# A hybrid attention and mLSTM encoder layer: background stores, weight sums and loads queued behind each projection's last evacuation and its store

## The chip, the cores and the metric

The kernel runs on one core of a Trainium2 chip. Five engines matter: TensorE (PE) multiplies matrices out of SBUF into PSUM, VectorE (DVE) and ScalarE (ACT) do elementwise work and empty PSUM, GpSimd (POOL) does a little, and SyncE (SP) issues nearly all DMAs between the device's memory (HBM) and SBUF. Each engine works through its own queue in order. The metric is the device time of one execution in microseconds (us).

## The reference

One encoder layer is applied to two sequences, a prompt of 1024 tokens and a sample of 2048, with 16 learned meta tokens in front, model width 1024. Cut to what matters here:

```python
xn = _rmsnorm(h, g_pre)
proj = xn @ w_in + b_in                       # 1024 x 6672, all float32
na_q, na_k, na_v, na_z, ml_qk, ml_v, ml_z, ml_o, ml_g, mg = split(proj)
ya = (neighbourhood_attention(na_q, na_k, na_v, na_rpb) * silu(na_z)) @ w_a
yb = (mlstm_branch(ml_qk, ml_v, ml_g, ml_o, ml_conv_w, ml_head_g) * silu(ml_z)) @ w_b
ga, gb = split(sigmoid(mg))
out = h + _rmsnorm((ga * ya + gb * yb) @ w_out, g_post)
```

## The kernel before, in words

**Numbers.** Float32 products are made of three passes: each operand is split into a high part (rounded by a copy on ScalarE) and a low part (the rest, by a subtraction on VectorE), and `mm3` (lines 182 to 187) issues high x high, low x high and high x low. For weights the parts are `whi` and `wlo`, for the normalised tokens `xh` and `xl`.

**Dense and sparse work.** The projections, the output stage and the gates are the dense stream (`dense`, line 1922); the mLSTM (`ml`) and the neighbourhood attention (`na`) are the sparse stream (`sparse`, line 1969). `run` interleaves the two, so that TensorE has projection matmuls to do while the other stream's chain of small steps goes on. The order of TensorE's instructions is that in which they are written. On all other engines the framework's scheduler chooses the order of each queue from a simulated timeline: an instruction that is written late but depends on nothing can stand early in its queue. `tc.issue_after(x)` limits that: what is written in its block on the engine of x is queued behind x. It adds an order of issue and no wait for a result.

**PLAN** (line 41) lists the groups of the dense stream: (sequence, first token, columns), columns m for the mLSTM's, n for the attention's, g for the gates'; the entries with f are the final stages. A group covers 1024 tokens in two halves of 512. `group` (line 936) works in jobs: four blocks of 128 columns, each by `fm_half` for the first half and then the second. `fm_half` (line 647) makes 24 matmuls into one PSUM bank (two banks with meta tokens) and yields four times; then `fm_evac` (line 600) empties the bank on VectorE and ScalarE into a tile `st` (4 buffers) and stores that to HBM from SP (lines 631 to 639). PSUM has three banks `pj` for this. `tm_unit` (line 676) does the same for columns whose tokens lie on partitions, two yields to a block.

**Turns.** After each yield of `group` and `sgates`, `beside` (line 523) counts a turn and does a piece of background work. A turn has 6 matmuls of 512 columns or 12 of 256. The first group takes 166 turns, the first two 298, the first three 458. The first job of the first group is the four columns of the mLSTM's q (tensors `mq`), turns 1 to 32; the second its gate z. Columns of z are evacuated by two ACT steps and one VectorE step (lines 620 to 622).

**Background work.**
- *Stores of x.* The sparse order of PLAN comes back to a half later, so `xkeep` (line 514) queues 16 stores of 256 KB for each half of 512 tokens, the eight slices of `xh` and of `xl`, in `xput`. `beside` issues one at every fourth turn (line 528). `xparts` (line 354) hands out new buffers for x; before that it issues all that is still in `xput` (line 356), since the buffers of the half before last are reused.
- *wprep* (line 537), the block sums of the gate weights. The gates of two groups are computed by a seven-product block scheme (`sgates`, line 859), which needs sums of blocks of the weights. For each of 8 pairs of column blocks wprep loads 2 x 512 KB of raw weights (`pr`, line 549), yields three times, and then four times makes a tile `po`: a copy on ACT (line 562), a subtraction on VectorE (line 563), two stores of 512 KB (tensors q, line 566), two yields; two of the four have VectorE sums before them and one more yield. `pr` and `po` have one buffer each. This is 13 steps to a pair, 104 in all. One step is taken at every second turn from turn 28, and at every eighth from the sixth pair on.
- *tprep* (line 570), block sums of x for the same scheme, in groups (1, 1024, n) and (1, 0, n): at every third turn a step of VectorE and ACT work on tiles `xr`, with stores to the tensors T.
- *tload* (line 837): six loads of 1 MB of T. In the gate group (1, 1024, g), `sgates` takes one at a time between its first projections.
- *build_half* (line 442) prepares the next half of x: loads of tokens (`xr`), sums of squares (line 331), loads of the transposed tokens (`xt`), the split. It isn't under `beside`.

`held` (line 167) looks up the last instruction written on VectorE and on ScalarE, of whatever kind, and queues its block behind these two. It surrounds the store of x in `beside`, and the loads of T in `sgates`; both are SP instructions. wprep and tprep run outside of it.

The weights themselves (`wload`, `wpump`, `wflush`, lines 249 to 307) come from `wu` at the first use, are split, and their two parts are stored (`wh`, `wl`); later groups load these.

Of the kernel before, what the change touches and what calls it, by code (L numbers as in the profile page):

```python
# [20 lines left out]
KT = D // P  # L21
# [114 lines left out]
class K:  # L136
# [3 lines left out]
    def __init__(self, tc, ins, outs):  # L140
        self.tc, self.nc = tc, tc.nc
        self.xs = []
        self.i, self.o = ins, outs
        self.wreq, self.wraw, self.wrdy, self.wout = deque(), deque(), deque(), 0
        self.wseen, self.wkept, self.xkept = set(), {}, {}
        self.rwait = {}
        self.xput, self.turn, self.last, self.turns = deque(), 0, None, False
        self.need = False
        self.hold, self.early = deque(), True
        self.side, self.qd, self.TD = None, {}, {}  # L150
# [15 lines left out]
    @contextmanager  # L166
    def held(self):

        with ExitStack() as st:
            left = {mybir.EngineType.DVE, mybir.EngineType.Activation}  # L170
            for x in reversed(self.nc.cur_bb.bb.instructions):
                if x.engine in left:
                    left.remove(x.engine)
                    st.enter_context(self.tc.issue_after(x))
                    if not left:
                        break
            yield

    def psum(self, tag, shape):
# [172 lines left out]
        self.nc.scalar.activation(out, p, AF.Copy)  # L352

    def xparts(self):
        while self.xput:
            self.nc.sync.dma_start(*self.xput.popleft())
        return [self.wp.tile([P, KT, HALF], F32R, name=n, bufs=2) for n in ("xh", "xl")]

# [83 lines left out]
    def build_half(self, s, t0, res):  # L442

        nc, wp = self.nc, self.wp
        if (s, t0) in self.xkept:
            yield
            yield "scaled"
            x = []
            for name, part in zip(("xh", "xl"), self.xkept[s, t0]):
                x.append(wp.tile([P, KT, HALF], F32R, name=name, bufs=2))  # L450
                for k in range(0, KT, 4):
                    nc.sync.dma_start(x[-1][:, k:k + 4, :512].bitcast(F32), part[:, k:k + 4, :])
                yield
            res.append(tuple(x))
            return
        if s == 0:
            xts = self.xnext
            self.xnext = None
            while self.rwait:
                yield "wait"  # L460
            self.early = False
            yield "scaled"
            g = self.gpre
            p = self.psum("sm", [P, 512])
            nc.tensor.matmul(p[:, :KT], self.ident, g, start=True, stop=True)
            g = self.cp.tile([P, KT], F32, name="gx")
            nc.vector.tensor_copy(g, p[:, :KT])
            x, r = self.xparts(), []
            for e in range(4):
                self.xsplit(x, xts[e], e, 0, g)  # L470
                self.wflush(2)
                yield
            res.append(tuple(x))
            self.xkeep(s, 0, self.xs[0], NM)
            self.xkeep(s, t0, x)
            yield from self.rsum(self.toks, r)
            nc.vector.tensor_copy(self.rc[:, 4:8], r[0])
            dg = self.rdiag(r[0], self.toks[0][0])

            def rows():  # L480
                self.rrows(dg, self.rr[:, 1], "sm")
                self.RD = self.dp.tile([P, D], F32, name="rrd")
                nc.sync.dma_start(self.RD[:, :], self.rr.rearrange("p a t -> p (a t)"))
                self.xp.close()
                self.side, self.pace = self.wprep(), 2
            self.rwait[s, t0] = rows
        else:
            bp = self.bp
            toks, r = self.tokens(s, t0, range(4), bp, 4), []
            yield  # L490
            yield from self.rsum(toks, r)
            dg = self.rdiag(r[0], toks[3][0])
            xts = [self.xtload(s, t0, e, bp, 4) for e in range(3)]
            yield
            rr = bp.tile([P, 512], F32, name="rx", tag="thT", bufs=1)
            self.rrows(dg, rr, "pj")
            xts.append(self.xtload(s, t0, 3, bp, 4))
            yield
            for k in range(KT):
                v = xts[k // 2][:, k % 2]  # L500
                nc.vector.scalar_tensor_tensor(v, v, self.gpre[:, k:k + 1], rr, op0=ALU.mult, op1=ALU.mult)
                if k % 2:
                    yield
            yield "scaled"
            x = self.xparts()
            for e in range(4):
                h = x[0][:, 2 * e:2 * e + 2, :512]
                nc.scalar.activation(h, xts[e], AF.Copy)
                nc.vector.tensor_tensor(x[1][:, 2 * e:2 * e + 2, :512], xts[e], h.bitcast(F32), op=ALU.subtract)
                yield  # L510
            res.append(tuple(x))
            self.xkeep(s, t0, x)
# [10 lines left out]
    def beside(self):  # L523

        self.turn += 1
        if self.xput and self.turn % 4 == 1:
            with self.held():
                self.nc.sync.dma_start(*self.xput.popleft())
        if self.side and self.turn % self.pace == 0 and next(self.side, "end") == "end":
            self.side = None  # L530

    def drain(self):
        while self.side:
# [3 lines left out]
    def wprep(self):  # L537

        nc = self.nc
# [2 lines left out]
        self.pq = ExitStack()  # L542
        pool = self.pq.enter_context(self.tc.tile_pool(name="pq", bufs=1, side="right", reuse_waits="tile"))
        for p in range(8):
            if p == 5:
                self.pace = 8
            raw = pool.tile([P, 2, 2, 512], F32, name="pr", bufs=1)
            for f in range(2):
                nc.sync.dma_start(raw[:, f].rearrange("p a c -> p (a c)"), self.i["wu"][unit["i", C_GA + (2 * p + f) * P, P], :, :D])
            for _ in range(3):  # L550
                yield
            for f, ops in ((0, ("11", "12")), (1, ("21", "22")), (1, ("s3", "s1")), (0, ("s2", "s4"))):
                if ops[0] == "s3":
                    nc.vector.tensor_tensor(raw[:, 1, 1], raw[:, 1, 0], raw[:, 1, 1], op=ALU.add)
                    sub(raw[:, 1, 0], raw[:, 0, 0], raw[:, 1, 0])
                    yield
                if ops[0] == "s2":
                    sub(raw[:, 0, 0], raw[:, 1, 1], raw[:, 0, 0])
                    sub(raw[:, 0, 1], raw[:, 0, 1], raw[:, 0, 0])
                    yield  # L560
                o = pool.tile([P, 2, 2, 512], F32R, name="po", bufs=1)
                nc.scalar.activation(o[:, :, 0], raw[:, f], AF.Copy)
                sub(o[:, :, 1], raw[:, f], o[:, :, 0].bitcast(F32))
                for q, op in enumerate(ops):
                    d = self.qd[p, op] = self.dp.tile([P, D], F32, name=f"q{p}{op}")
                    nc.sync.dma_start(d[:, :], o[:, q].rearrange("p a c -> p (a c)").bitcast(F32))
                yield
                yield
# [31 lines left out]
    def fm_evac(self, col, s, t0, meta, chunks, ps):  # L600

        nc, wp = self.nc, self.wp
        bi = (col // P) if col < 4608 else 36 + (col - 4624) // P
        bias = self.bfm[:, bi:bi + 1]
        st = wp.tile([P, HALF], F32, name="st", bufs=4)
        m = NM if meta else 0
        n = 512 + m
# [19 lines left out]
        if C_MQ <= col < C_MV:  # L627
            dst = (self.MQ if col < C_MK else self.MK)
            h = (col % 512) // P
            lo = 0 if meta else NM + t0  # L630
            nc.sync.dma_start(dst[s][h][:, lo:lo + n], st[:, :n])
            if meta:
                nc.sync.dma_start(dst[1 - s][h][:, :NM], st[:, :NM])
            return
        if col >= C_GA:
            dst = self.GT[s][(col - C_GA) // P]
        else:
            dst = (self.NQ, self.NK, None, self.NZ, None, None, None, self.SZ)[col // 512][s][(col % 512) // P]
        nc.sync.dma_start(dst[:, t0:t0 + 512], st[:, m:n])
        if meta and C_NK <= col < C_NV:  # L640
            km = wp.tile([P, 64], F32, name="km", bufs=1)
            nc.gpsimd.memset(km, 0.0)
# [33 lines left out]
    def tm_unit(self, col, halves, wd):  # L676
# [10 lines left out]
        for j, (x, s, c, n, cnt, tok) in enumerate(todo):  # L687
            st = self.bp.tile([P, 2, WU], F32, name="stT", bufs=4)
            for a in range(cnt):
# [17 lines left out]
                        yield (8 if tok is None else 12) * C256  # L707
                if j == len(todo) - 1 and a == cnt - 1:
                    self.wdone()
                if tok is None:  # L710
                    nc.scalar.activation(st[:n, 1, :wd], p[2 * NM:2 * NM + n, :wd], AF.Copy)
                    nc.vector.tensor_tensor(st[:n, 1, :wd], p[:n, :wd], st[:n, 1, :wd], op=ALU.add)
# [5 lines left out]
                    nc.vector.tensor_tensor(st[:n, a, :wd], p[:n, :wd], bb[:n, :wd], op=ALU.add)  # L718
                if a == cnt - 1:
                    self.tm_store(col, wd, s, n, cnt, tok, st)  # L720
                yield (8 if tok is None else 12) * C256

    def tm_store(self, col, wd, s, n, cnt, tok, st):
# [135 lines left out]
    def sgates(self, s, t0, lead, nxt):  # L859
# [3 lines left out]
        for hf in range(2):  # L863
            if hf == 0:
                ws = [self.wtake(1)[0] for _ in range(2 * len(lead))]
            for u, w in enumerate(ws):
                if hf or u > 1:
                    with self.held():
                        next(more, None)
                p, f = lead[u // 2], u % 2  # L870
                yield from self.fm_half(C_GA + (2 * p + f) * P, w, self.xs[hf], s, t0 + 512 * hf, False, done=self.wdone if hf else None)
# [1194 lines left out]
```

## Time and profile before

| | us |
|---|---|
| median of 3 runs | 2782.44 (2778.36 to 2783.21) |
| the profiled execution's own time | 2780.05 |
| its span (first to last instruction) | 2778.2 |
| TensorE busy in it | 2704.1 |
| VectorE busy | 1877.6 |
| ScalarE busy | 1388.7 |

The profile shows one execution. A row of instructions names the line, the engine, what is written and read (out<-in), how many (x), and how long the engine stood idle before it and what ended that idle time ([us <-releaser]). PEld is TensorE's loading of weights, which overlaps the matmuls. SPq, ACTq and DVEq are the engines' sequencers; SPq with DMA_DIRECT2D is the issue of a DMA, not its transfer. The DMA share is the mean busy share of the core's 16 DMA engines, and PEclk the clock that TensorE was granted, 1.00 being full speed. All places are in us from the start of the span.

### The profile page before, as it was taken

The page shows a single profiled execution, that of the slowest core. Times are in us where ns is not written, and L with a number is a line of the kernel's source. Part 1 is how long each engine was busy: PE and PEld are TensorE (multiplying, and loading weights), DVE is VectorE, ACT ScalarE, POOL GpSimd, SP SyncE. Part 2 cuts the span into 40 slices and gives each one's busy share as a digit, 9 for nine tenths or more (in the row PEclk, how much of TensorE's full clock was granted, in tenths as well). Part 3 has the DMA queues.
Part 4 walks back from the last instruction along what each step waited for, and adds up shares of the span by engine and source line. Part 5 has one row for each costly group of instructions (what it writes and reads, how often), then busy time and mean ns, then how long its engine had stood idle before and what let it go on. Part 6 is the DMA issues. An engine that isn't in the chain of part 4 may idle for free.

```text
span 2778.2 us, 47366 instructions
## 1 busy us (share of the span) xinstructions
PE 2704.1 (97%) x16144; PEld 2380.2 (86%) x16144; DVE 1877.6 (68%) x5174; ACT 1388.7 (50%) x3302; POOL 17.9 (1%) x100
## 2 busy tenths in 40 slices
PE   9699899999999999999999999999999999999998
PEld 7599798889878998898798887887888989899898
DVE  5343588866768666368867665674668798887844
ACT  5332464653446555346546564562455556555421
POOL 0000000000000000000000000000000000000000
PEclk9899999999999999999999999999999999999999
DMA  9978887965599655679969889989549898989975
GB/s 367 365 291 306 301 309 263 368 222 174 199 363 319 207 188 181 206 227 340 319 227 314 278 260 362 320 256 330 166 152 313 255 316 251 344 261 299 304 254 208
DMA packets 397539, 762.76 MB, mean 275 GB/s; under 512 B 50192, under 2 KB 179168, under 8 KB 395760
## 3 DMA queue, kind: packets, MB, share of 16 engines
q1 hardware_dynamic: 396176, 757.04, 80.1%
q0 software_dynamic: 1120, 2.69, 0.4%
q8 instruction: 128, 2.10, 0.3%
q14 instruction: 115, 0.94, 0.1%
HBM read 514.89 MB, written 244.69 MB: 273 GB/s over the span
## 4 chain that ended last, share of the span: by engine, by line
PE 50%; DMA 3%; DVE 2%; ACT 0%; issue 0%; SPq 0%; DVEq 0%; ACTq 0%
PE pj L185 7%; PE pj L187 7%; PE pj L186 7%; PE pj L1827 3%; PE pj L1829 3%; PE pj L1828 3%; PE pj L891 3%; PE pj L893 3%; PE pj L892 3%; PE sm L1176 2%; PE tr L1161 2%; DMA whi<-q 1%; PE pj L701 1%; PE pj L702 1%; PE pj L703 1%; DMA t2h<-t2h 0%
## 5 line engine op out<-in xcount | busy, mean ns | idle before, releaser
L185 PE MATMUL pj<-xh,whi 128*128 128x512 f32 (+1 forms) x1376 | 543.5, 395 | 29.4 <-ACT st L621 21.1
L186 PE MATMUL pj<-xl,whi 128*128 128x512 f32 (+1 forms) x1376 | 529.2, 385 | 0.4 <-DVE xl L366 0.4
L187 PE MATMUL pj<-xh,wlo 128*128 128x512 f32 (+1 forms) x1376 | 528.5, 384 | 0.8 <-DMA wlo<-wl 0.5
L701 PE MATMUL pj<-whi,xh 128*128 128x256 f32 (+1 forms) x1152 | 329.2, 286 | 0.0
L185 PEld LDWEIGHTS pj<-xh,whi 128*128 128x128 f32 x1376 | 263.0, 191 | 74.7 <-ACT st L621 21.6
L702 PE MATMUL pj<-wlo,xh 128*128 128x256 f32 (+1 forms) x1152 | 324.8, 282 | 0.0
L703 PE MATMUL pj<-whi,xl 128*128 128x256 f32 (+1 forms) x1152 | 324.7, 282 | 0.0
L187 PEld LDWEIGHTS pj<-xh,wlo 128*128 128x128 f32 x1376 | 261.9, 190 | 55.9 <-DMA wlo<-wl 1.6
L186 PEld LDWEIGHTS pj<-xl,whi 128*128 128x128 f32 x1376 | 262.9, 191 | 41.8 <-issue 1.0
L1827 PE MATMUL pj<-whi,mh 128*128 128x256 f32 x768 | 217.2, 283 | 0.4 <-DMA whi<-wh 0.4
L701 PEld LDWEIGHTS pj<-whi,xh 128*128 128x128 f32 x1152 | 217.0, 188 | 0.4
L702 PEld LDWEIGHTS pj<-wlo,xh 128*128 128x128 f32 x1152 | 217.0, 188 | 0.1
L703 PEld LDWEIGHTS pj<-whi,xl 128*128 128x128 f32 x1152 | 217.0, 188 | 0.0
L1829 PE MATMUL pj<-whi,mlo 128*128 128x256 f32 x768 | 216.8, 282 | 0.0
L1828 PE MATMUL pj<-wlo,mh 128*128 128x256 f32 x768 | 216.7, 282 | 0.0
L1168 DVE TENSOR_TENSOR pts<-tr,pts 96x384 fp32r<-96x384 f32 (+2 forms) x192 | 118.8, 619 | 70.5 <-ACT pts L1163 68.9
L1163 ACT ACTIVATE pts<-tr 96x384 fp32r<-96x384 f32 (+2 forms) x192 | 103.4, 539 | 106.9 <-PE tr L1161 106.0
L185 PE MATMUL pj<-yh,whi 128*128 128x512 f32 x384 | 154.9, 403 | 0.0
L187 PE MATMUL pj<-yh,wlo 128*128 128x512 f32 x384 | 151.3, 394 | 0.0
L186 PE MATMUL pj<-yl,whi 128*128 128x512 f32 x384 | 150.8, 393 | 0.0
L1827 PEld LDWEIGHTS pj<-whi,mh 128*128 128x128 f32 x768 | 145.4, 189 | 1.5 <-DMA whi<-wh 0.6
L1828 PEld LDWEIGHTS pj<-wlo,mh 128*128 128x128 f32 x768 | 145.4, 189 | 1.0
(363 smaller groups left out, 6112.8 us busy)
## 6 DMA issues: line engine op xcount, KB each, us to landing
whi<-wh SPq DMA_DIRECT2D x160, 512.0 KB
wlo<-wl SPq DMA_DIRECT2D x160, 512.0 KB
wraw<-wu SPq DMA_DIRECT2D x48, 512.0 KB
wh<-whi SPq DMA_DIRECT2D x48, 512.0 KB
wl<-wlo SPq DMA_DIRECT2D x48, 512.0 KB
gt<-st SPq DMA_DIRECT2D x96, 256.0 KB
tg<-gt SPq DMA_DIRECT2D x96, 256.0 KB
whi<-q SPq DMA_DIRECT2D x45, 512.0 KB
```

Of the source, the lines that this page charges most:

```text
L185: mm(out, ah, bh, start=start, stop=False)
L186: mm(out, ah, bl, start=False, stop=False)
L187: mm(out, al, bh, start=False, stop=stop)
L701: nc.tensor.matmul(o, xh, wh, start=k == 0, stop=False)
L702: nc.tensor.matmul(o, xh, wl, start=False, stop=False)
L703: nc.tensor.matmul(o, xl, wh, start=False, stop=k == KT - 1)
L891: mm(bank, w[:, 0, k], xh[:, k], start=fresh and k == 0, stop=False, skip_group_check=True)
L1163: nc.scalar.activation(pts[:ks, :nb, 0, :], pt[:ks, :nb], AF.Copy)
L1168: self.nc.vector.tensor_tensor(pts[:ks, :nb, 1, :], pt[:ks, :nb], pts[:ks, :nb, 0, :].bitcast(F32), op=ALU.subtract)
L1827: nc.tensor.matmul(o, mh[:, k, xs], wh, start=clear > 0 and k == 0, stop=False)
L1828: nc.tensor.matmul(o, mh[:, k, xs], wl, start=False, stop=False)
L1829: nc.tensor.matmul(o, ml[:, k, xs], wh, start=False, stop=clear < 2 and k == KT - 1)
```

## The change

Five edits:

1. `mark` remembers the last instruction on VectorE, ScalarE and SP among those that an evacuation and its store have just written (in `fm_evac` and `tm_unit`). `behind` queues its block behind these three.
2. The stores of x in `beside` are under `behind` instead of `held`; they start after turn 36 and come at every sixth turn up to turn 280 and at every third after it, instead of every fourth.
3. `xparts` issues only what is over 16 stores; the last half's 16 may stay queued.
4. The steps of wprep and tprep are under `behind`. wprep's pace is a step every fourth turn throughout.
5. The loads of T in `sgates` are under `behind` instead of `held`.

```diff
@@ K.__init__
+        self.marks = {}
+    def mark(self, start):
+
+        for x in self.nc.cur_bb.bb.instructions[start:]:
+            if x.engine in (mybir.EngineType.DVE, mybir.EngineType.Activation, mybir.EngineType.SP):
+                self.marks[x.engine] = x
+
+    @contextmanager
+    def behind(self):
+
+        with ExitStack() as st:
+            for x in self.marks.values():
+                st.enter_context(self.tc.issue_after(x))
+            yield
@@ xparts
-        while self.xput:
+        while len(self.xput) > 2 * KT:
@@ build_half
         if (s, t0) in self.xkept:
+            assert not self.xput
...
-                self.side, self.pace = self.wprep(), 2
+                self.side, self.pace = self.wprep(), 4
@@ beside
-        if self.xput and self.turn % 4 == 1:
-            with self.held():
+        if self.xput and self.turn > 36 and self.turn % (6 if self.turn < 280 else 3) == 1:
+            with self.behind():
                 self.nc.sync.dma_start(*self.xput.popleft())
-        if self.side and self.turn % self.pace == 0 and next(self.side, "end") == "end":
-            self.side = None
+        if self.side and self.turn % self.pace == 0:
+            with self.behind():
+                if next(self.side, "end") == "end":
+                    self.side = None
@@ wprep
-            if p == 5:
-                self.pace = 8
@@ fm_evac, and the same around the evacuation and store in tm_unit
+        start = len(nc.cur_bb.bb.instructions)
...
+        self.mark(start)
@@ sgates
-                    with self.held():
+                    with self.behind():
                         next(more, None)
```

More of the change, by code (lines that the diff above doesn't have):

```diff
@@ L639, in fm_evac @@
         nc.sync.dma_start(dst[:, t0:t0 + 512], st[:, m:n])
+        self.mark(start)
         if meta and C_NK <= col < C_NV:
@@ L709, in tm_unit @@
                     self.wdone()
+                start = len(nc.cur_bb.bb.instructions)
                 if tok is None:
@@ L720, in tm_unit @@
                     self.tm_store(col, wd, s, n, cnt, tok, st)
+                self.mark(start)
                 yield (8 if tok is None else 12) * C256
```

## The prediction, made before the result was known

> **What bounds the kernel now.** I read the page's busy times first, then TensorE's waits, then a table of stretches around each wait.
>
> ```profile
> span 2778.2 us, 47366 instructions
> PE 2704.1 (97%) x16144; PEld 2380.2 (86%) x16144; DVE 1877.6 (68%) x5174; ACT 1388.7 (50%) x3302; POOL 17.9 (1%) x100
> ```
> ```profile
> PE pj L185 <- ACT st L621: 21.1, 1, 21.1
> PE tr L1448 <- DVE kf L1412: 7.4, 2, 4.2
> PE pj L185 <- DMA wlo<-q: 5.5, 2, 3.1
> PE pj L185 <- DMA whi<-wh: 4.2, 2, 3.8
> PE tr L1708 <- DVE hb L1703: 4.1, 2, 2.3
> PE pj L185 <- ACT st L626: 3.1, 1, 3.1
> ```
>
> TensorE is the bound: it stands only 2778.2 - 2704.1 = 74 us. The change adds and removes no matmul, and TensorE's order is fixed by hand, so all that can be won is this idle time and the slow matmuls behind it; all that can be lost is new waits. One wait of 21.1 us is over a quarter of the idle time. The stretches around the waits (columns: length; busy us of PE, PEld, DVE, ACT, POOL; granted clock; DMA share; GB/s):
>
> ```profile
> 57.90:65.00 7.10, 3.95 (x12) 3.14 (x12) 1.92 (x2) 2.97 (x4) 0.00 (x0) 0.76 0.84 302
> 79.40:106.00 26.60, 5.46 (x15) 4.25 (x15) 6.48 (x19) 9.84 (x17) 0.52 (x7) 0.62 1.02 399
> 318.00:348.00 30.00, 22.19 (x140) 20.42 (x140) 21.15 (x51) 16.53 (x39) 1.85 (x6) 0.89 1.00 353
> 438.00:458.00 20.00, 14.95 (x81) 12.69 (x80) 14.44 (x49) 8.99 (x23) 0.00 (x0) 0.83 0.80 275
> 769.00:785.00 16.00, 11.35 (x40) 7.85 (x39) 0.75 (x1) 1.37 (x2) 0.00 (x0) 0.89 1.04 405
> 1346.00:1356.00 10.00, 7.73 (x29) 5.87 (x28) 9.09 (x26) 3.71 (x9) 0.00 (x0) 0.83 1.05 383
> 1699.00:1724.00 25.00, 19.55 (x76) 15.72 (x75) 5.26 (x19) 6.00 (x15) 0.00 (x0) 0.80 1.04 402
> 1910.00:1942.00 32.00, 27.80 (x115) 21.89 (x114) 12.04 (x38) 7.38 (x12) 0.00 (x0) 0.95 0.86 268
> ```
>
> The reader is to see that nearly every wait falls where the DMA share is about 1, and that the clock drops behind each. I price a stretch as length minus PE's busy time, plus (1 - clock) times length for the slow matmuls.
>
> **The opening (79.4 to 106).** Why is the evacuation late?
>
> ```profile
> L528 SPq DMA_DIRECT2D xh<-xh x16: 319/368/600, 31.7 to 65.3; - x16
> L528 SPq DMA_DIRECT2D xl<-xl x16: 319/440/1236, 44.8 to 72.7; - x16
> xh<-xh SPq DMA_DIRECT2D x16, 256.0 KB
> pr<-wu SPq DMA_DIRECT2D x2, 512.0 KB
> 40.00:75.00 35.00, 0.95 0.99 372
> 77.87 0.70 SPq L549 DMA_DIRECT2D pr<-wu  x1
> 91.61 3.15 SPq L631 DMA_DIRECT2D mq<-st  x4
> 99.08 0.69 ACT L620 ACTIVATE st<-pj,bfm 128x512 f32<-128x512 f32 x1 [10.04 <-DMA mq<-st]
> ```
>
> ACT could evacuate only at 99.08, when a store of mq had landed and given back an st buffer; the four stores were issued at 91.61. SP issues in order into DMA engines that are full (share 0.99, 372 GB/s). Ahead of those stores stand 32 stores of x (8.4 MB) and two loads of wprep's raw weights (1.05 MB): 9.4 MB / 372 GB/s = 25.4 us. held() orders VectorE and ScalarE only, so it never kept an SP store back: all 32 are out by 72.7. The change removes both kinds from this place. The stores of x come after turn 36, behind the store of an evacuation. wprep's first step falls on turn 32 and stands behind the last store of mq. That brings 91.61 to about 66 and 99.08 to about 74 (the fourth evacuation is itself not before 72). TensorE asks for the bank at 79.5, so the cover is some 5 us.
>
> ```profile
> 100.70:105.10 4.40, 4.40 (x11) 3.44 (x12) 2.01 (x3) 2.53 (x4) 0.00 (x0) 0.50 1.01 409
> 105.10:109.50 4.40, 4.40 (x20) 3.58 (x19) 0.93 (x2) 1.20 (x2) 0.00 (x0) 1.00 0.77 303
> 61.00:64.10 3.10, 3.00 (x7) 2.43 (x8) 0.00 (x0) 1.42 (x3) 0.00 (x0) 0.50 0.95 350
> ```
>
> The wait costs more than itself: 11 matmuls in 4.4 us behind it, 20 in the next 4.4, so 9 x 0.22 = 2.0 us; behind the 3.1 us wait, 1.5 us likewise. At stake: 21.1 + 2.0 + 3.1 + 1.5 = 27.7. I keep 4 as left over, since other early loads may move up: **-24**. Bounds: -27.7, and -8 if about half the bytes are replaced by others (25.4 / 2 = 12.7 us earlier, 8.4 of the 21.1 left, much of the rest unsure).
>
> The Trainium skill (TensorE: Matmul & The Clock Gate, Part 1) says that the clock halves after an idle window of about 3.4 us. Here a longest gap of 2.3 us at 1348 already has a clock of 0.83 around it, so the trace differs; by the page's figure the shorter gaps would cost only themselves and my whole sum would be about 6 us smaller.
>
> **Where the stores of x go.** 32 stores at every sixth turn from 37 end at turn 223. Turn 32 ends at 57.9 and turn 458 (first three groups of PLAN) at 770, the two gaps above; by proportion turn 223 is about 377 us. They bring 8.4 MB / 307 us = 27 GB/s there.
>
> ```profile
> 110.00:300.00 190.00, 190.00 (x1312) 176.19 (x1311) 89.45 (x150) 57.72 (x79) 0.00 (x0) 1.00 0.82 304
> 300.00:460.00 160.00, 146.61 (x974) 133.84 (x973) 120.21 (x330) 86.26 (x205) 4.00 (x16) 0.96 0.87 306
> 460.00:760.00 300.00, 298.94 (x1824) 264.49 (x1822) 216.46 (x671) 161.58 (x411) 3.73 (x18) 1.00 0.70 236
> ```
>
> From 110 to 300 TensorE never stands, at 304 of 372 GB/s, and wprep, which now runs at half its rate, takes away more than that (next part: 117 to 61 GB/s). Cost 0; bounds 0 and +22.6 (every byte as dear as in the opening); the row is nearest to 0.
>
> **wprep, pace 4 throughout.** 8 passes of 13 steps, 104 steps, 416 turns from turn 28: it ends near turn 444, some 747 us, instead of 447.
>
> ```profile
> L562 ACT ACTIVATE po<-pr x32: 1040/1060/1064, 88.0 to 447.2; 128x1024 fp32r<-128x1024 f32 x32
> L541 DVE TENSOR_TENSOR po<-pr,po x32: 1208/1224/1227, 89.1 to 448.3; 128x1024 fp32r<-128x1024 f32 x32
> 437.25 1.06 ACT L562 ACTIVATE po<-pr 128x1024 fp32r<-128x1024 f32 x1 [3.37 <-DMA q<-po]
> 447.19 1.06 ACT L562 ACTIVATE po<-pr 128x1024 fp32r<-128x1024 f32 x1 [4.09 <-DMA q7s<-po]
> ```
>
> A pass moves 1.05 MB of raw weights in and 4.2 MB of sums out, so the 8 passes are 42 MB: over the 359 us from 88 to 447 they are 117 GB/s, over some 690 us 61 GB/s. Today the copies po come as fast as their one buffer allows, and ACT stands in front of them with the mLSTM's copies queued behind. Two such waits lie just ahead of TensorE's gaps in 438 to 458, which cost 5.1 + 3.4 = 8.5; 318 to 348, with the same work around it, costs 7.8 + 3.3 = 11.1. From 300 to 460 there are 32 x 160 / 359 = 14 copies now and 32 x 160 / 690 = 7 after: half of 19.6 back, **-9** (bounds 0 and -19.6). In exchange about 13 copies move into 460 to 760: ACT 13 x 1.06 = 14 us; VectorE 13 x 1.22 and as many half-size sums of about 0.6 (estimated from the 1.22) = 24 us; 13 / 32 of 42 MB, 57 GB/s. Shares there go from 72 to 80% on VectorE, from 0.70 to about 0.87 on DMA. Bounds: 0, and 300 x (13.4 / 160) = +25, if the stage then stands as 300 to 460 does now. I take **+10**, nearer the low end, because a copy now has two steps, 8 turns or 48 matmuls at 0.22 = some 11 us, for its buffer's stores. No semaphore is added: behind() fixes issue order only. On SP the loads pr and the stores of x now queue behind a store that waits for its evacuation; only po waits for them, 12 turns later.
>
> **The later stores of x, tprep, the loads of T.**
>
> ```profile
> 747.00 1.29 SPq L528 DMA_DIRECT2D xh<-xh  x3
> 770.21 4.17 SPq L356 DMA_DIRECT2D xl<-xl  x5
> L582 DVE TENSOR_TENSOR xr<-xh,xl x16: 1209/1217/1226, 794.7 to 1359.2; 128x1024 f32<-128x1024 f32 x16
> 1678.45 0.54 SPq L847 DMA_DIRECT2D t1l<-t1l  x1
> 1703.78 1.13 SPq L272 DMA_DIRECT2D wlo<-q  x1
> ```
>
> At 747 to 774 stores of x go out in a burst, partly flushed by xparts, beside the loads of whi that TensorE lacks at 770. They become one per three turns and 16 may stay back. That stretch costs 4.7 + 1.8 = 6.5: **-4** (0 to -6.5). tprep's additions and subtractions fill VectorE at 1346 (9.09 of 10 us); behind evacuations at pace 3 they spread: 2.3 + 1.7 = 4.0, **-3** (+4 to -4: some of them ran 270 us earlier than traced, from 794.7, and now can't). At 1678 the six loads of T, 1 MB each by the code, pass ahead of the wlo that TensorE lacks; then they go behind the evacuations of the first lead projections. That stretch costs 5.5 + 5.0 = 10.5, but the same 6.3 MB (17 us at 372 GB/s) come some 30 us later and nearer their use: **-4** (-10.5 to +10). The 1910 stretch waits for nothing that moves: 0.
>
> **Sum:** -24 + 0 - 9 + 10 - 4 - 3 - 4 = -34. The profiled execution took 2780.05 (span 2778.2 and 1.9 around it), 2.4 under the median of 2782.44: **2746 us**.
>
> **The rivals.**
> 1. The opening is won, the rest is repaid: the new order makes as many small waits as it removes. For it: VectorE at 75% and DMA at 0.87 from 300 to 460 sufficed for 13.4 us. Then -24 + 10 = -14: 2766.
> 2. All the listed waits go: -27.7 - 19.6 - 6.5 - 4 - 10.5 = -68: 2712. Against it: DMA stays near 1 in three of these stretches whatever the order.
> 3. Slower: po blocks ACT. A copy right behind an evacuation that still waits for its load or its buffer's stores holds up the next evacuation. Place: 460 to 760. Price: two such waits went with 8.5 us, so 4.2 each. Thirteen of them are 55 us in place of my 10: -44 + 55 = +11, 2791. It decides from (34 + 10) / 4.2, ten or eleven blocked copies. Against it: the 11 us between copies are more than the 7.5 us from issue (91.61) to release (99.08) in the worst stretch. The Trainium skill (Perfetto Trace Analysis, Per-engine timelines) calls the queues of ACT and DVE strict first-in first-out, which speaks for this rival; the two po rows agree.
> 4. It doesn't do what it says: held() already failed to hold an SP store, and if other hoisted loads fill the freed queue, the stores of mq stay late: about 2780.
>
> **How the numbers follow.** Forecast (2735 to 2760) 0.52; rival 1 (2760 to 2776) 0.20; rival 2 (2712 to 2735) 0.12; rival 3 0.11; rival 4 0.05. The range, 2720 to 2780, leaves out the far half of rival 2 and rival 3. About 0.2%, 5.6 us, is what a measurement of this kernel can tell from no change: faster 0.84, same 0.05, slower 0.11.
>
> **What would show it.** Right: no store of x before about 70 us, the four stores of mq issued near 66 to 75, TensorE's wait at 79.5 under 5 us, PE busy in 57.9 to 84 nearly throughout. po from about 70 to 750 us, with few ACT waits before it. The stores of x at even distances. Wrong: ACT waits at po of 3 us or more in 460 to 760 with TensorE gaps behind them; a wait of L891 for t1 to t3 near 1720; or a wait at 79.5 that names another transfer.

## The result, and the profile after

| | before | after |
|---|---|---|
| median, us | 2780.78 (2778.36 to 2783.21) | 2732.76 (2731.13 to 2734.76) |
| the profiled execution's own time | 2780.05 | 2734.13 |

Both medians are of four runs. The ratio is 0.9828, with a 95% interval of 0.9811 to 0.9845: 48 us faster by the medians, 45.9 by the two profiled executions. In the changed kernel the matmuls of the projections are at lines 200 to 202 (before: 185 to 187) and most other lines are 15 to 21 higher.

The page of after, its first lines, and TensorE's waits (us in total, times, longest):

```profile
span 2732.4 us, 47321 instructions
PE 2691.8 (99%) x16144; PEld 2372.7 (87%) x16144; DVE 1877.1 (69%) x5174; ACT 1389.1 (51%) x3302; POOL 16.7 (1%) x100
```
```profile
PE tr L1469 <- DVE kf L1433: 6.1, 2, 4.3
PE sc L1598 <- DVE nwy L160: 6.0, 1, 6.0
PE sc L1150 <- ACT kd L1128: 2.9, 2, 2.2
PE sm L202 <- DVE ktl L1473: 2.6, 3, 1.8
```

VectorE and ScalarE are as busy as before to within 1 us: no work has gone. TensorE's idle time fell from 74.1 to 2732.4 - 2691.8 = 40.6 us, the rest of the 45.9 is slow matmuls that are gone. The wait of 21.1 us for `st` has left the list; two waits for kf, together 6.1 us, and one wait of 6.0 lead it. Those for kf have namesakes in before, at 322 and 338; in after they fall at 1149 (4.3 us) and 1726 (1.7).

TensorE's 16144 matmuls stand in the same order in both kernels. So a stretch of before is compared with the stretch of after that holds the same matmuls, and the difference in length is what was won or lost there. The windows of after that match the stretches of before (the matmul count, x in the PE column, differs by one at most from cutting):

```profile
56.30:80.90 24.60, 24.60 (x107) 19.91 (x106) 8.84 (x23) 10.82 (x18) 0.52 (x7) 1.00 1.03 413
289.00:308.90 19.90, 19.47 (x141) 18.25 (x140) 13.68 (x35) 11.09 (x28) 0.62 (x3) 1.00 1.01 371
398.80:410.60 11.80, 11.80 (x82) 10.80 (x81) 10.81 (x32) 6.79 (x18) 0.00 (x0) 1.00 0.81 262
410.60:462.10 51.50, 44.73 (x197) 36.04 (x196) 40.38 (x93) 31.88 (x71) 0.51 (x4) 0.90 0.83 299
733.10:743.20 10.10, 9.29 (x41) 7.22 (x40) 0.75 (x1) 1.38 (x2) 0.00 (x0) 1.00 1.04 408
1058.00:1167.90 109.90, 102.19 (x576) 87.62 (x575) 62.94 (x167) 46.74 (x111) 0.79 (x12) 0.97 0.74 248
1313.00:1318.70 5.70, 5.70 (x28) 4.71 (x27) 3.48 (x12) 2.42 (x5) 0.00 (x0) 1.00 0.80 281
1661.50:1676.40 14.90, 14.90 (x76) 12.39 (x75) 5.01 (x20) 5.00 (x12) 0.00 (x0) 1.00 1.02 363
1676.40:1727.80 51.40, 47.06 (x227) 37.44 (x226) 27.95 (x91) 23.50 (x65) 0.10 (x1) 1.00 1.01 377
```

The partners in before that the prediction didn't show:

```profile
57.00:109.50 52.50, 28.21 (x106) 22.01 (x105) 10.73 (x25) 15.14 (x24) 0.67 (x8) 0.77 0.97 368
458.00:500.10 42.10, 41.79 (x198) 33.65 (x197) 35.09 (x77) 27.99 (x64) 0.40 (x3) 1.00 0.80 281
1100.00:1200.00 100.00, 99.54 (x575) 85.63 (x575) 44.72 (x142) 40.38 (x102) 0.89 (x13) 1.00 0.64 217
1724.00:1770.00 46.00, 45.55 (x227) 37.65 (x226) 29.13 (x101) 26.40 (x75) 0.10 (x1) 1.00 0.97 329
```

The opening's 106 matmuls take 24.6 us instead of 52.5. The stretches of 318, 438, 769, 1346 and 1699 are each 4 to 10 us shorter. Three stretches in which before hardly waited (under 0.5 us each) are longer: 458 to 500 by 9.4, 1100 to 1200 by 9.9, 1724 to 1770 by 5.4. By the start of the same matmul in both traces, the lead of after grows like this (us; places in before's time):

| stretch | predicted | measured |
|---|---|---|
| opening, up to 200 | +24 | +28.8 |
| 318 to 348 and 438 to 458 (wprep) | +9 | +10.2 and +8.4 |
| 460 to 760 | -10 | -9.6 up to 500, then -1.7 |
| 769 to 785 (stores of x) | +4 | +6.0 |
| 785 to 1100 | 0 | 0.0 |
| 1100 to 1200 | 0 | -9.9 |
| 1346 to 1356 (tprep) | +3 | +4.1 |
| 1699 to 1770 (loads of T) | +4 | +10.2, then -5.5 |
| all else | 0 | +4.9 |
| sum | +34 | +45.9 |

How the opening came free: the SP queue of after (start, us, what is issued), and the two ScalarE steps that matter:

```profile
61.84 2.78 SPq L648 DMA_DIRECT2D mq<-st  x3
...
71.75 0.69 SPq L648 DMA_DIRECT2D mq<-st  x1
72.49 0.94 SPq L565 DMA_DIRECT2D pr<-wu  x2
75.46 0.33 SPq L657 DMA_DIRECT2D sz<-st  x1
75.83 0.44 SPq L544 DMA_DIRECT2D xh<-xh  x1
```
```profile
70.06 0.69 ACT L637 ACTIVATE st<-pj,bfm 128x512 f32<-128x512 f32 x1 [3.35 <-DMA mq<-st]
...
81.45 1.06 ACT L578 ACTIVATE po<-pr 128x1024 fp32r<-128x1024 f32 x1 [1.16 <-DMA pr<-wu]
```

The stores of mq now start at 61.84 instead of 91.61, and the evacuation that started at 99.08 starts at 70.06. The first store of x follows at 75.83, behind all four. The DMA engines are as full as ever (share 1.03, 413 GB/s in the first window above), and TensorE never stops.

### The profile page after: what moved, and what is told of

Its sections match the earlier page's. It is cut to its first block, busy times and chain, and to the rows that moved or that the text cites. A ratio compares the mean times of both kernels' runs of the same rounds, so it can differ in the third digit from the quotient of the medians.

```text
span 2732.4 us, 47321 instructions
## 1 busy us (share of the span) xinstructions
PE 2691.8 (99%) x16144; PEld 2372.7 (87%) x16144; DVE 1877.1 (69%) x5174; ACT 1389.1 (51%) x3302; POOL 16.7 (1%) x100
## 4 chain that ended last, share of the span: by engine, by line
PE 87%; DMA 7%; DVE 3%; ACT 2%; issue 1%; SPq 0%; DVEq 0%; ACTq 0%
PE pj L200 14%; PE pj L202 13%; PE pj L201 13%; PE pj L720 5%; PE pj L722 5%; PE pj L721 5%; PE pj L1849 3%; PE pj L1848 3%; PE pj L1850 3%; PE pj L912 3%; PE pj L914 3%; PE pj L913 3%; PE sm L1197 3%; PE tr L1182 3%; DMA va<-mv 1%; DMA whi<-q 1%
```

## The experiments

Each edit is made to the changed kernel. Ratios are to before on the same chip, whose medians were 2778.59, 2778.24 and 2775.47.

**1. The stores of x as held() places them.** Theory: the opening was lost to what stood ahead of mq's stores in SP's queue. Rival: the new cadence, not the queue, does it.

```diff
-            with self.behind():
+            with self.held():
                 self.nc.sync.dma_start(*self.xput.popleft())
```

> The changed kernel with the stores of x under held() again, at their new turns (after 36, every sixth). Theory (queue order): held() puts no order on SP, so the stores of x written at turns 37 to 223 move up to 30 to 75 us, stand ahead of the four stores of mq as before, and TensorE's wait near 79 us is back with 15 us or more; with the slow matmuls behind it about 25 us lost, some 2758 us. Rival (timing): the later turns alone keep the stores out of the opening; no wait over 5 us there, 2733 us.

Measured: 2765.67 (2764.25 to 2769.88), ratio 0.9953 (0.9937 to 0.9970). TensorE's waits, and SP:

```profile
PE pj L200 <- ACT st L638: 17.0, 1, 17.0
...
PE pj L200 <- DMA whi<-wh: 5.8, 1, 5.8
PE pj L200 <- ACT st L643: 4.8, 2, 4.2
```
```profile
88.65 4.12 SPq L648 DMA_DIRECT2D mq<-st  x4
```

The cadence is that of after, and yet the stores of x start at 34.1 us, the stores of mq wait until 88.65 and the long wait is back. The lead at 200 is 2.4 us instead of 28.8. SP's order is the cause; the cadence falls. At 769 the wait for `whi` returns too (2.6 us lost instead of 6.0 won).

**2. The stores of x at once, every fourth turn.** Is the threshold of turn 36 needed?

```diff
-        if self.xput and self.turn > 36 and self.turn % (6 if self.turn < 280 else 3) == 1:
+        if self.xput and self.turn % 4 == 1:
```

> The changed kernel with the stores of x under behind(), but at the old turns (every fourth from the start, no threshold of 36). Theory (queue order): behind() lets out only one store for each four turns, about 5 of them (1.3 MB, 3.5 us at 372 GB/s) ahead of the last store of mq, so TensorE's wait near 79 us stays under 5 us: 2733 to 2740 us. Rival (timing): the threshold of 36 is what frees the opening; the wait is back with over 15 us, 2755 us or more.

Measured: 2735.62 (2732.4 to 2739.35), ratio 0.9843 (0.9825 to 0.9862). The lead at 200 is 28.2. Neither the threshold nor the slower cadence matters to the opening: `behind` is enough. (This run loses 4.7 us more than after between 500 and 760; the medians don't tell the two kernels apart.)

**3. wprep and tprep not behind anything.** Is edit 4's gain the queueing or the pace? (The pace stays at 4.)

```diff
-            with self.behind():
-                if next(self.side, "end") == "end":
-                    self.side = None
+            if next(self.side, "end") == "end":
+                self.side = None
```

> The changed kernel with wprep and tprep outside of behind(), paces kept (4 and 3). Theory: wprep's place is set by its pace, so its copies po still run until about 700 us and nothing changes before 760; tprep moves back up to about 760, the new waits at 1100 to 1200 (9.9 us lost there in the changed kernel) go, and the 4 us won at 1313 (1346 of before) are lost again: about 2727 us. Rival: behind() is what spreads wprep; without it the copies are all done by about 450, the 18.6 us won between 318 and 458 of before are lost: 2745 us or more.

Measured: 2732.84 (2729.21 to 2738.74), ratio 0.9835 (0.9814 to 0.9856): the same as after, and 6 us more than the 2727 expected. wprep's two stretches win 10.8 and 8.0, about as in after. That isn't because its copies stay where they were, as the expectation had it. Without `behind` the last one starts at 478.9 instead of 703.2:

```profile
L577 ACT ACTIVATE po<-pr x32: 1039/1059/1066, 67.7 to 478.9; 128x1024 fp32r<-128x1024 f32 x32
```

So the queueing moves wprep's copies by over 200 us, and at this pace the time doesn't change. tprep goes back to its early place, and the stretch of 1100 takes as long as in before (its window):

```profile
1063.80:1163.90 100.10, 99.64 (x577) 85.77 (x576) 44.73 (x142) 40.33 (x102) 0.80 (x12) 1.00 0.64 215
```

Against after, that is 9.9 won; but 4.4 are lost at 1346, 5.0 at 769, 3.2 at 1200 to 1346 and 2.4 at 458 (the profiled run is the longest of the four). By the medians the queueing of the two is a wash. Not all of these losses are tprep's: the 5.0 at 769 don't come back in experiments 10 and 11, where its first run is early too.

**4. The same, and wprep at its old pace** (2, from the sixth pair on 8).

```diff
-                self.side, self.pace = self.wprep(), 4
+                self.side, self.pace = self.wprep(), 2
+            if p == 5:
+                self.pace = 8
```

> The changed kernel with wprep as before: pace 2, then 8 from the sixth pair on, and outside of behind() (tprep too). The stores of x stay queued. Theory (crowding): 32 copies po by about 450 us bring back waits like those at 318 to 348 and 438 to 458 of before, 10 to 20 us, while the 9.6 us lost at 458 to 500 go; tprep as in sums_free; a first load pr ahead of the stores of mq costs up to 3 us in the opening: 2735 to 2745 us. Rival: those two waits hung on the order that the opening's stall left behind, not on wprep's rate; they stay away, 2718 to 2730 us.

Measured: 2747.85 (2745.13 to 2748.96), ratio 0.9884 (0.9865 to 0.9903). That is more than the 2735 to 2745 expected. 318 to 348 is still won (10.8), but 9.4 of it is repaid up to 400, and 438 to 458 is won by 0.5 only. One TensorE wait and ScalarE's queue at that place:

```profile
PE sc L1599 <- ACT kh L1561: 5.4, 1, 5.4
```
```profile
333.39 0.69 ACT L1571 ACTIVATE um<-um,g_a 128x128 f32<-128x128 f32 x2 [0.24 <-DVE um L1569]
333.99 1.04 ACT L579 ACTIVATE po<-pr 128x1024 fp32r<-128x1024 f32 x1
334.94 0.40 ACT L1561 ACTIVATE kh<-kf 128x256 fp32r<-128x256 f32 x1
```

A copy of po stands between two mLSTM steps, and TensorE waits for the second; the copy itself is 1.04 of the 5.4 us. Experiment 3 differs from this one in wprep's written pace alone, and the old pace costs 17 us in these stretches (9.4 and 7.5), 15.0 by the medians. But the copies are hardly more crowded here than there:

```profile
L579 ACT ACTIVATE po<-pr x32: 1039/1058/1075, 67.2 to 456.9; 128x1024 fp32r<-128x1024 f32 x32
```

Counted at TensorE's places, 13 copies start between 300 and 460 of before in before itself, 12 here, 10 in experiment 3 and 6 in after. So it isn't their number that decides; that it is the place where single copies fall fits the rows above, and no run shows it alone.

This run also says something of the opening: wprep's two loads of raw weights are issued at 56.05 and 61.31 again, ahead of mq's last four stores (63.79 to 74.26), and the lead at 200 is still 27.9. Taking the stores of x out of the queue was enough.

**5. The old pace, but behind the evacuations.**

```diff
-                self.side, self.pace = self.wprep(), 4
+                self.side, self.pace = self.wprep(), 2
+            if p == 5:
+                self.pace = 8
```

> The changed kernel with wprep at pace 2 and then 8, but still under behind(). Theory (crowding by rate): five of eight passes at the old rate, so the mLSTM waits at 318 to 400 of before are back as in pace_free (about 9 us net), but the last three passes can't run early, so 8 us stay won at 438 to 458: about 2741 us. Rival: behind() alone keeps the copies from blocking; 2733 us.

Measured: 2743.94 (2737.91 to 2747.99), ratio 0.9887 (0.9868 to 0.9906). 348 to 400 loses only 1.8, and 438 to 458 wins 8.4. So these two stretches are won by either means, the new pace or the place in the queue, and the gains don't add. But the kernel is 12.7 us slower than after on the same chip (2731.23, experiments 10 and 11). By the profiled runs the rest of that lies elsewhere (2.1 in the opening, 3.1 at 769, 2.1 at 785, 3.9 at 1100); why the old pace should cost there was not taken apart. ScalarE does stand before copies of po here, nine times for 1.3 to 5.2 us between 130 and 258, and TensorE loses nothing in that stretch.

**6. `xparts` issues all that is left** (edit 3 undone). Theory: in before, the burst of stores of x at half changes held the token loads behind it back, and so kept the squares made from them out of the way of the mLSTM's q; without the burst the squares come first, and TensorE waits at 446 us of after.

```diff
-        while len(self.xput) > 2 * KT:
+        while self.xput:
```

> The changed kernel with xparts issuing all queued stores of x again (edit 3 undone). It tells why all four kernels so far lose 9 us at the place of 458 to 500 of before (a wait of mLSTM's sc for q). Theory (order of ScalarE): the flush of 16 stores used to push the loads of tokens back on SP and in the scheduler's timeline; without it the four squares of the next half stand ahead of the copy of q on ScalarE. With the flush back the 9.6 us come back, the burst at 733 may cost up to 6: 2723 to 2730 us. Rival: the loss hangs on something else that all four share; 2733 us or more.

Measured: 2734.51 (2734.46 to 2736.42), ratio 0.9845 (0.9830 to 0.9859). 458 to 500 still loses 8.0, so this theory fell. 769 to 785 wins 1.5 instead of 6.0: edit 3 is worth 4.5 us there, and next to nothing in all.

**7. The loads of T as held() places them.**

```diff
-                    with self.behind():
+                    with self.held():
                         next(more, None)
```

> The changed kernel with the loads of T under held() again (edit 5 undone). Theory: the six loads stand ahead of the wlo of the first lead projection again, the 10.2 us won at 1699 to 1724 of before are lost, the 5.5 us lost at 1724 to 1770 come back: 4 to 5 us more, 2737 us. Rival: the gain at 1699 came from the general shift of the DMAs; no change, 2733 us.

Measured: 2738.15 (2733.84 to 2741.73), ratio 0.9855 (0.9841 to 0.9870). The wait and the window with the same 76 matmuls:

```profile
PE pj L200 <- DMA wlo<-q: 7.0, 2, 3.6
```
```profile
1661.90:1687.30 25.40, 18.37 (x76) 14.84 (x75) 5.72 (x20) 6.00 (x15) 0.00 (x0) 0.87 1.04 401
```

The two waits for `wlo` are back (25.4 us instead of 14.9), and the 5.5 us lost behind them in after shrink to 0.4. The order of these loads is worth 5 us net. What is lost behind is not mainly a wait for T: of TensorE's waits from 1676 to 1728 of after, 1.7 us are for kf, 1.5 for vwh and 0.6 for a tile of T.

**8. x as before: edits 2 and 3 undone together.** What do edits 4 and 5 bring alone?

```diff
-        while len(self.xput) > 2 * KT:
+        while self.xput:
-        if self.xput and self.turn > 36 and self.turn % (6 if self.turn < 280 else 3) == 1:
-            with self.behind():
+        if self.xput and self.turn % 4 == 1:
+            with self.held():
```

> The changed kernel with everything about the stores of x as before (edits 2 and 3 undone: held(), every fourth turn, xparts issues all). It asks which edit makes the wait of sc for q (9 us lost at 458 to 500 of before), which x_held and flush_all alone did not remove and which pace_free has too. Theory: the stores of x, hoisted and flushed together, kept the token loads and so the squares back; with both as before the loss goes, the opening is lost as in x_held: about 2760 us. Rival: wprep's pace or place makes it as well; the loss stays, 2770 us.

Measured: 2764.66 (2763.05 to 2768.34), ratio 0.9963 (0.9950 to 0.9976). Edits 4 and 5 bring 2775.47 - 2764.66 = 10.8 us, the stores of x 2764.66 - 2731.23 (after beside it on the same chip, experiments 10 and 11) = 33.4. The lead at 200 is 1.8; 458 to 500 still loses 7.4.

**9. build_half behind evacuations as well.** Of the wait at 446 the trace shows who is in front: ScalarE in after, ahead of the copy of the mLSTM's q (L1551),

```profile
445.68 1.06 ACT L346 ACTIVATE xsq<-xr 128x1024 bf16<-128x1024 f32 x1 [1.56 <-DMA xr<-x_sample]
...
447.66 1.04 ACT L346 ACTIVATE xsq<-xr 128x1024 bf16<-128x1024 f32 x1
...
449.84 1.05 ACT L346 ACTIVATE xsq<-xr 128x1024 bf16<-128x1024 f32 x1
...
450.88 0.41 ACT L1551 ACTIVATE q<-cv 128x256 fp32r<-128x256 f32 x1
```

and the same place in before:

```profile
487.62 1.06 ACT L331 ACTIVATE xsq<-xr 128x1024 bf16<-128x1024 f32 x1 [2.44 <-DMA xr<-x_sample]
...
490.74 1.05 ACT L331 ACTIVATE xsq<-xr 128x1024 bf16<-128x1024 f32 x1
...
491.78 0.41 ACT L1530 ACTIVATE q<-cv 128x256 fp32r<-128x256 f32 x1
```

All four of build_half's squares stand ahead of the q copy in after (the first at 440.31), two of them in before (the other two follow at 495.80 and 497.76), and TensorE waits 5.98 us for `sc<-q,kh` (the row of waits names a constant, nwy; in x_held it names q). So build_half's steps are put behind evacuations:

```diff
-                            side()
+                            with self.behind():
+                                side()
```

> The changed kernel with the preparation of the next half of x (build_half's loads, squares and splits) under behind() as well. Theory: the 6 us wait of sc for q at 446 us comes from four squares of 1.06 us that stand ahead of the copy of q on ScalarE and wait for tokens; written behind evacuations, one to a step, they no longer stand together: the 9.6 us lost there come back, and the token loads leave the opening: about 2723 us. Rival: the splits of x now come later than TensorE needs them, and it waits for xh at the start of a group: 2740 us or more.

Measured: 2773.19 (2768.96 to 2778.65), ratio 0.9981 (0.9969 to 0.9993): nearly the whole gain is gone. TensorE's first waits:

```profile
PE pj L366 <- DMA vr<-nv: 11.3, 1, 11.3
PE pj L366 <- ACT xr L358: 10.6, 2, 7.9
PE pj L366 <- DMA xt<-xt: 9.2, 1, 9.2
...
PE sc L1599 <- DVE q L1553: 4.5, 2, 3.4
```

build_half has matmuls of its own (the row of scales, L366), which stand at a fixed place of TensorE's order; its steps now come too late for them, 31 us in all. The wait for q is 3.4 instead of 6.0, but TensorE comes to it behind one of these waits (7.9 us), and 458 to 500 as a whole loses 14.9 instead of 9.6. So this run doesn't tell whether the squares were to blame. Work that TensorE itself waits for is no background work.

**10 and 11. tprep behind evacuations only in its second run, and after again beside it.** Experiment 3 says that tprep's queueing costs at 1100 and gains at 1346; the first is its first run, the second its second.

```diff
-        self.marks = {}
+        self.marks, self.loose = {}, False
-            with self.behind():
+            with self.behind() if not self.loose else ExitStack():
                 if next(self.side, "end") == "end":
-            self.side, self.pace = self.tprep(s, t0), 3
+            self.side, self.pace, self.loose = self.tprep(s, t0), 3, t0 > 0
```

> The changed kernel with the first tprep (group 1, 1024, n) outside of behind(), the second inside. Theory: each tprep costs or pays where it runs: the 9.9 us lost at 1100 to 1200 of before go as in sums_free, about 5 of the 6 us won at 769 to 785 go too, the 4.1 us at 1346 stay: about 2728 us. Rival: the small waits roll anew with every edit and no such sum holds; 2733 us or more.

Measured: 2723.95 (2722.79 to 2730.19), ratio 0.9809 (0.9795 to 0.9824). 1100 to 1200 loses 0.6, 1346 wins 4.1, as expected. The gain at 769, most of which was expected to go, stays (6.3); 2.7 are lost behind it, up to 900. Then, on one chip, the changed kernel and this one:

> The changed kernel itself, on the same chip as the next one: 2733 us.

> tprep2 again, beside the changed kernel on the same chip. Theory (the first tprep belongs where VectorE and DMA have room): 8 to 10 us under the changed kernel in the same runs, 2724 us. Rival: the difference was one of chips; under 3 us.

Measured: 2731.23 (2728.45 to 2736.66), ratio 0.9845 (0.9831 to 0.9860), for after; 2727.36 (2725.09 to 2731.25), ratio 0.9831 (0.9816 to 0.9845), for the other, 3.9 us less. The stretch of 1100 comes out as before both times (0.0 lost here, 11.3 in after beside it), but at 1500 to 1600 the profiled run lost 3.5. The ranges overlap: the version is probably the better one, by 4 us on one chip and 5 by the ratios on different chips, and that isn't settled.

## Why the prediction was right, and where it was not

The forecast was 2746 with a range of 2720 to 2780; the time is 2732.76. It said that most of the gain is the opening, and so it is.

**The opening** is right in mechanism and place. It was predicted that mq's stores would be issued near 66 and the late evacuation would start at 74; they are issued at 61.84 (three) and 71.75 (the fourth), and it starts at 70.06. The 4 us kept as left over weren't needed: 28.8 against 27.7 at stake. x_held shows that the queue does it: the one word `held` for `behind` brings back 26.4 of the 28.8. One part of the account wasn't needed: the two loads of raw weights that it counted ahead of mq's stores may stay there (pace_free, 27.9).

**wprep** is the mis-sized term: half of 19.6 was taken back, 18.6 came. The prediction made the waits proportional to the copies between 300 and 460, 14 and then 7. The waits don't follow that number: from 318 to 458, after wins 18.5 with 6 copies there, sums_free 17.9 with 10, and pace_free 1.1 with 12. The new pace or the new place is enough for these stretches (sums_free, pace_2_8); with neither, 17 us are lost. In 438 to 458 the trace of before shows how: two copies, each after a wait of its own of 3 to 4 us, stand ahead of the mLSTM's kth, for which TensorE waits. For 318 to 348 it doesn't. Weight copies and evacuations stand between the copies of po and the two waits for kf, and even pace_free, with wprep as before, wins this stretch and loses 9.4 in the next. That these 10.2 us are wprep's is not shown. The copies themselves, in after:

```profile
L578 ACT ACTIVATE po<-pr x32: 1041/1054/1071, 81.5 to 703.2; 128x1024 fp32r<-128x1024 f32 x32
...
  DMA q<-po: 5.8, 4
```

ScalarE waits 5.8 us for q's stores, 4 times, instead of 20.3, 11 times, in before.

**460 to 760** came out as written (10 predicted, 11.3 measured) by luck, for another reason. The charge was for 13 copies of po and their sums; but 9.6 of the loss lie at 458 to 500, where ScalarE squares build_half's tokens ahead of the q copy. The loss is there in every kernel of this study, with the stores of x as before (7.4) and with wprep's pace as before (8.7). Every one of these kernels reaches that place some 20 us or more earlier than before does. The loads of x_sample, which the squares wait for, come earlier too, but not always by as much: in after they are issued 44.6 to 47.0 us earlier, where TensorE is 46.6 ahead; in x_as_before 16.6 to 19.5, where it is 20.6 ahead. These shortfalls, of 4 us at most, are less than what is lost. No run tested it, and the cause stays open. Rival 3, po blocking ScalarE, didn't happen: after 460, ScalarE stands only once before a copy of po for q's stores, for 2.5 us.

**The stores of x at 769** (6.0 against 4) and **the loads of T** (4.7 against 4) went about as described: flush_all takes away 4.5 of the first, t_held all of the second. The exchange in the second was foreseen as a saving at `wlo` and a later cost, and both are in the windows; but the later cost is mostly the mLSTM's small waits (kf, vwh) and not waits for T.

**tprep** is the step that failed. Predicted: 3 won at 1346, with a bound of +4 for additions that "ran 270 us earlier than traced, from 794.7, and now can't". Measured: 4.1 won at 1346 and 9.9 lost at 1100. The first of its additions in after:

```profile
L598 DVE TENSOR_TENSOR xr<-xh,xl x16: 1161/1217/1227, 966.8 to 1365.4; 128x1024 f32<-128x1024 f32 x16
```

They start 172 us later and fall among the mLSTM's loads and convolutions, where TensorE waits 4.3 us for kf; the step ahead of kf on ScalarE waits for a load:

```profile
1150.99 0.51 ACT L1356 ACTIVATE cv<-raw,cw 128x256 f32<-128x256 f32 x1 [2.18 <-DMA raw<-mk]
```

That the loss is tprep's is shown (sums_free and tprep2 both remove it, and it is there in each kernel that keeps tprep's first run behind evacuations); whether its copies, its VectorE sums or its stores (eight, issued from 1136 to 1167) do the harm was not taken apart. The bound was too small: it allowed 4 us for the work that moves, and not for the chain into which it moves.

Of the rivals, "all the listed waits go" (2712) came closest on the gains, and "the rest is repaid" on the costs: the stretches that were listed gave back 28.8 + 18.6 + 6.0 + 4.1 + 10.2 = 67.7 of its 68, and 9.6 + 9.9 + 5.5 = 25 were paid at new places.

## What to carry to other kernels

An order among instructions holds only on the engines that it names: a DMA that "belongs behind" an evacuation must be put behind that evacuation's own store on the queue that issues both; here the scheduler hoisted it otherwise, and the late stores cost 26 us. Background work beside a chain of small steps is worth placing or pacing anew, and here either won back the same stretches; it must not include what the bound engine itself waits for. When work is moved, look at the chain that runs where it arrives: three stretches with hardly a wait in before gave back 25 of the 68 us that were won.

## What the runs showed of the hardware

Full DMA engines alone cost nothing in the opening. From 56.3 to 80.9 of after their share is 1.03 at 413 GB/s, more than the 0.97 and 368 GB/s of the same matmuls in before, and TensorE is busy throughout.

Some short gaps slow the clock. Behind a TensorE wait of 1.73 us at 1871 of after (two stretches of 3.4 us, the wait in the first):

```profile
1871.30:1874.70 3.40, 1.67 (x9) 1.19 (x9) 2.81 (x12) 0.30 (x1) 0.00 (x0) 1.00 1.02 393
1874.70:1878.10 3.40, 3.40 (x10) 2.66 (x9) 0.00 (x0) 0.38 (x1) 0.00 (x0) 0.50 0.52 201
```

The clock is 0.50 in the second stretch. Not every such gap does this: behind the 1.71 us at 1726 of after and behind 1.84 us at 1914 of before the granted clock stays 1.00 for the next 6.8 us. What separates them isn't shown. The Trainium skill (TensorE: Matmul & The Clock Gate, Part 1) gives an idle window of about 3.4 us as what lowers it. This trace doesn't agree: it shows half the clock behind a gap of half that length, as the prediction had supposed from the gap at 1348 of before.
